# A decoder trunk in fp32 on one core: the address of three tiles in the SwiGLU, and the PSUM bank of one gate product

## The chip, the core and the metric

The kernel runs on one core of a Trainium2 chip. TensorE (PE) multiplies a moving tile of up to 512 columns with a stationary tile of 128 by 128 that a weight load (PEld) has put into it; results go to PSUM, here eight banks of 128 x 512 float32. VectorE (DVE), ScalarE (ACT) and GpSimd (POOL) work on tiles in SBUF, and DVE and ACT also read PSUM. DMAs are issued by SyncE's queue (SP), and some by POOL and ACT.

The metric is the device time of the whole program in microseconds. The median of three runs before the change is 1161.38 us (1160.37 to 1162.3).

## What is computed

One sequence of 512 tokens with 1,024 features passes a recurrent layer and an attention layer, each with a SwiGLU behind it. Only the recurrent mixer and the SwiGLU concern the change:

```python
def rg_lru(x, w_a, b_a, w_x, b_x, lam):
    ...
    r_gate = jax.nn.sigmoid(jnp.einsum('bshi,hij->bshj', xb, w_a.astype(jnp.float32)).reshape(B, S, C) + b_a.astype(jnp.float32))
    i_gate = jax.nn.sigmoid(jnp.einsum('bshi,hij->bshj', xb, w_x.astype(jnp.float32)).reshape(B, S, C) + b_x.astype(jnp.float32))
    log_a = -LRU_C * r_gate * jax.nn.softplus(-lam.astype(jnp.float32))
    a = jnp.exp(log_a)
    u = jnp.sqrt(-jnp.expm1(2.0 * log_a)) * (i_gate * x32)
...
def swiglu(h, w_in, w_out):
    g, u = jnp.split(h @ w_in, 2, axis=-1)
    return (jax.nn.silu(g) * u) @ w_out
```

The gates multiply each of eight blocks of 128 channels with a 128 x 128 matrix of its own, twice. The SwiGLU has a hidden width of 2,816.

## The kernel before

**Products.** The float32 result is kept by splitting each operand into a high and a low float32r part and adding three products: high with high, high with low, low with high. `mm3` (lines 164 to 168) issues them; its argument `w` is the stationary pair, `x` the moving pair. The profile names a matmul as out<-moving,stationary: `ps<-wh,T` has the tile `wh` moving and a slice of a tile `T` stationary.

**The recurrent layer.** Sixteen blocks of the input projection (`in_block`, 24 matmuls each) run in the order of `lru_order`: first the eight of the x branch (here projection blocks 0 to 7), then the eight of the y branch (8 to 15). Each takes a PSUM bank. `bank()` without a tag hands out the three banks `mm` and the bank `X` in turn; projection blocks 0, 1, 2 thus have `mm`, block 3 has `X`, and block 4 asks for `PT`, of which there are two. Blocks 5, 6, 7 have `mm`, block 8 `X` again. `x_block` (line 444) reads a projection block out of its bank with DVE, scales it into `xp`, and then come four taps of a convolution (lines 448 to 454: the first on ACT or POOL, three on DVE). `x_parts` splits the result into `xch` and `xcl`. `x_gates` (line 472) multiplies it with the two gate matrices, `pr` and `pi`, three matmuls each, and ACT reads them with a sigmoid (lines 482 and 484). Before the change `pr` has the bank `S` or `O` by turns and `pi` one of the two `PT`. The gates of blocks 0 and 1 follow projection block 5, those of 2 and 3 follow 6, those of 4 and 5 follow 8, those of 6 and 7 follow 9. ACT's sigmoids and exponentials are tied into runs (`act_order`), so that it changes its table seldom. The rest of this layer's order is made by a planner with estimates of its own, which may put parts of a projection block between the gates.

**The SwiGLU.** `swiglu` (line 578) is called twice, with the pool `ffn1` and with `ffn2`. The hidden blocks are computed by a scheme of seven products in place of eight (Strassen-Winograd), five times over (`ORDERS`): products with quarters of x as they lie in `xh` and `xl` (B11, B21, B22, T4), and three with sums and differences of x in the tiles `T1`, `T2`, `T3`. In each, slices of the x tile are stationary and the split weights `wh`, `wl` move; a product is 24 matmuls. Between them `out_block` (O) multiplies finished hidden chunks, `gh` and `gl` as moving tiles, with the output weights. At the end, T1 and T2 take the last hidden chunk, and eight blocks of 12 matmuls have them as moving tiles. In these stages the order of all five engines is written out by hand (`manual_schedule`).

**Where the tiles lie.** Pools lie one behind the other in a partition of SBUF, and in a pool the tiles lie in the order of their first call. Each number is an address in bytes in the partition, from the allocations:

| tile | begins at | remainder by 256 |
|---|---|---|
| h, xh, xl | 16,512; 32,896; 49,280 | 128 |
| wh and wl (three of 4,096 each) | 77,952; 90,240 | 128 |
| `gap` (128 bytes), ffn1 / ffn2 | 108,672 / 102,528 | 128 |
| T1, T2, T3 (8,192 each), ffn1 | 108,800; 116,992; 125,184 | 0 |
| T1, T2, T3, ffn2 | 102,656; 110,848; 119,040 | 0 |
| wt, the temporaries e, GA, GB, S1 | from 133,376 / 127,232 on | 0 |
| the norm's factors (`norm_factors`, 384 bytes), then S3, UB, rb, gh, gl | from 190,720 / 184,576 on | 128 from S3 on |

The tile `gap` is never read or written. It only takes up room.

Of the kernel before, what the change touches and what calls it, by code (L numbers as in the profile page):

```python
# [15 lines left out]
F32 = mybir.dt.float32  # L16
# [143 lines left out]
def trunk(tc, A, out):  # L160
# [3 lines left out]
    def mm3(ps, w, x, first, last, on=False):  # L164
        (wh, wl), (xh, xl) = w, x
        PE.matmul(ps, wh, xh, start=first, stop=False, skip_group_check=on)  # L166
        PE.matmul(ps, wh, xl, start=False, stop=False, skip_group_check=on)  # L167
        PE.matmul(ps, wl, xh, start=False, stop=last, skip_group_check=on)  # L168
# [55 lines left out]
    with tc.tile_pool(name="keep", bufs=1) as kp, tc.tile_pool(name="wts", bufs=3) as wp, \  # L224
# [6 lines left out]
        def bank(tag=None, name="ps"):  # L231
            tag = tag or next(rotation)
            return pp.tile([128, 512], F32, name=name, tag=tag, bufs={"mm": 3, "PT": 2}.get(tag, 1))
# [59 lines left out]
        def gain(c, k):  # L293
            return par[:, c + k:c + k + 1]
# [46 lines left out]
        with tc.tile_pool(name="lru", bufs=2) as lp, \  # L341
# [91 lines left out]
            def act_order(inst):  # L433

                for f in runs:
                    behind(tc, inst, f)
# [34 lines left out]

            def x_gates(b, xc, parts):
                c = slice(128 * b, 128 * b + 128)
                pr, pi = bank("SO"[b % 2]), bank("PT")
                for g, ps in enumerate((pr, pi)):
                    mm3(ps, (gwh[g][:, c], gwl[g][:, c]), parts, True, True)
                sl = slice(T * (b % 2), T * (b % 2) + T)
                if b % 2 == 0:
                    rate[b // 2] = lp.tile([128, 2 * T], F32, name="rate", bufs=4)
                    tau[b // 2] = lp.tile([128, 2 * T], F32, name="tau", bufs=4)  # L480
                r = rate[b // 2][:, sl]
                act_order(S.activation(r, pr, AF.Sigmoid, bias=gain(C_GA, b)))
                ig = lp.tile([128, T], F32, name="ig")
                act_order(S.activation(ig, pi, AF.Sigmoid, bias=gain(C_GX, b)))
                done.append(S.activation(tau[b // 2][:, sl], r, AF.Tanh, scale=sp4[:, b:b + 1]))
                V.tensor_tensor(gated[b], ig, xc, ALU.mult)
# [35 lines left out]
            for i, m in enumerate(lru_order):  # L522
                ps = first.pop(0) if first else in_block(p_in + i)

                if i in (5, 6, 8, 9):
                    for _ in range(2):
                        b = xs[0][0]
                        x_gates(*xs.pop(0))
                    if b % 4 == 3:
                        decays(b // 4)  # L530
                        decayed += range(b - 3, b + 1)
                        ready += 1
                if m < 8:
                    ys.append(y_block(m, ps))
                else:
                    xs.append(x_block(m - 8, ps))
                if i in (3, 5, 6, 8):
                    xs[:2] = [x_parts(*x) for x in xs[:2]]
                if i not in (6, 9):
                    for b in decayed[:2]:  # L540
                        recur(decayed.pop(0))
                while ys and ready == 2 and ys[0][0] < 8 - len(decayed):
                    y_gate(*ys.pop(0))
# [34 lines left out]
        def swiglu(fp, p, after, meanwhile=iter(())):  # L578
            ws.asp, ws.al = 2, 9
            temps = Temps(fp)  # L580
            fp.tile([128, 32], F32, name="gap", bufs=1)

            def chunk():
                return [fp.tile([128, 4, T], F32R, name=n, bufs=1) for n in ("gh", "gl")]
# [1 line left out]
            homes = {n: [x[:, 4 * k:4 * k + 4, 256 * t:256 * t + 256] for x in (xhs, xls)]  # L586
                     for n, k, t in (("B11", 0, 0), ("B21", 1, 0), ("B22", 1, 1), ("T4", 0, 1))}
            sums = [fp.tile([128, 4, T], F32R, name=f"T{i}", bufs=1) for i in range(1, 4)]
            for i, x in enumerate(sums):
                homes[f"T{i + 1}"] = [x[:, 2 * w:2 * w + 2].rearrange("q a (b t) -> q (a b) t", b=2) for w in range(2)]  # L590
            chunks = {}
# [233 lines left out]
        with tc.tile_pool(name="tables", bufs=1) as rp:  # L825
            rp = Pool(rp)
            with tc.tile_pool(name="ffn1", bufs=2) as fp:
                fp = Pool(fp)
                tables = []

                def make_tables():
                    tables.extend((yield from rotary(nc, A, rp, fp)))

                def after_f1(m, ps):
                    V.tensor_tensor(by_time(h[m]), by_time(h[m]), in_turn(ps), ALU.subtract)
                    split(h[m], gain(C_KV, m), xh[m], xl[m])
                    squares(m, Temps(fp))

                swiglu(fp, p_f1, after_f1, make_tables())


            with tc.tile_pool(name="att", bufs=2) as ap:
                ap = Pool(ap)
                attention(tc, A, ap, ws, dict(locals()))

        with tc.tile_pool(name="ffn2", bufs=2) as fp:
            fp = Pool(fp)

            def after_f2(m, ps):

                halves = [(slice(0, 2), nc.scalar), (slice(2, 4), nc.sync)]
                for c, queue in halves if m == 7 else [(slice(0, 4), nc.sync)]:
                    x = by_time(h[m])[:, :, c]
                    V.tensor_tensor(x, x, in_turn(ps)[:, :, c], ALU.subtract)
                    c = slice(128 * c.start, 128 * c.stop)
                    queue.dma_start(out[m][:, c], h[m][:, c])

            swiglu(fp, p_f2, after_f2)
# [534 lines left out]
```

## Time and profile before

| | |
|---|---|
| median of three runs | 1161.38 us |
| the profiled execution: time / its span | 1160.69 us / 1158.7 us |
| PE busy | 1150.0 us (99%) |
| DVE / ACT busy | 851.0 us (73%) / 622.9 us (54%) |
| granted clock of TensorE, mean | 1.00 |
| recurrent layer / first SwiGLU / attention / second SwiGLU | 0 to 156.5 / to 494 / to 824 / to 1158.7 us |

The span goes from the first to the last profiled instruction; the time of an execution holds some 2 us around it. Idle time of an engine counts only where the end waits for it, so the chain of work that ended last is read beside the busy times. A matmul's duration in the rows holds its way through the array, during which the next has begun already: how fast matmuls follow each other is read from their starts.

### The profile page before, as it was taken

What the parts mean: (1) busy time and instruction counts of PE and PEld (TensorE: products, weight loads), DVE (VectorE), ACT (ScalarE), POOL (GpSimd) and SP (SyncE); (2) the same over time, 40 slices, a digit from 0 to 9 for tenths busy, and PEclk for the clock granted to TensorE, in tenths of its full rate; (3) what the DMA queues carried; (4) which work ended last, traced back from release to release, by engine and by line L of the source; (5) the groups of instructions that cost most, each with busy time, mean ns of one, the idle gap of its engine ahead of it and who ended that gap; (6) DMA issues with size and microseconds to landing.
All of it is one profiled execution on the core that took longest, in us unless ns stands there. A gap on an engine that the chain in (4) does not pass through costs nothing.

```text
span 1158.7 us, 15131 instructions
## 1 busy us (share of the span) xinstructions
PE 1150.0 (99%) x5403; PEld 953.4 (82%) x5403; DVE 851.0 (73%) x1525; ACT 622.9 (54%) x901; POOL 187.7 (16%) x221
## 2 busy tenths in 40 slices
PE   9999999999999999999999999999999999999998
PEld 6788888888888888888888888798888888888886
DVE  8988688868777676887565667765888777676764
ACT  6797455553535353565555768665555435353531
POOL 4210010201001000020411234341102011010000
PEclk9999999999999999999999999999999999999999
DMA  7643366975666722432988658534668666657223
GB/s 243 154 113 110 103 226 161 241 202 153 185 167 180 183 74 82 122 108 88 222 185 174 156 104 198 119 74 110 222 160 231 193 162 188 171 167 194 76 76 124
DMA packets 92234, 179.61 MB, mean 155 GB/s; under 512 B 8704, under 2 KB 27008, under 8 KB 92160
## 3 DMA queue, kind: packets, MB, share of 16 engines
q1 hardware_dynamic: 72720, 130.80, 34.6%
q0 software_dynamic: 18864, 47.19, 23.2%
q8 instruction: 43, 0.70, 0.2%
q10 hardware_dynamic: 576, 0.66, 0.2%
q14 instruction: 31, 0.25, 0.1%
HBM read 164.99 MB, written 2.10 MB: 144 GB/s over the span
## 4 chain that ended last, share of the span: by engine, by line
PE 94%; DVE 2%; ACT 1%; issue 1%; POOL 0%; DMA 0%; SPq 0%; DVEq 0%; ACTq 0%
PE ps L168 25%; PE ps L167 25%; PE ps L166 25%; PE ps L1054 6%; PE ps L1055 6%; PE ps L1056 6%; PE ps L1222 1%; PE ps L1140 1%; DVE xc L454 1%; PE ps L299 0%; DMA wr<-in_w_in 0%; ACT pr L1208 0%; PE ps L1108 0%; ACT wh L117 0%; DVE wl L124 0%
## 5 line engine op out<-in xcount | busy, mean ns | idle before, releaser
L117 ACT CAST wh<-wr 128x1024 fp32r<-128x1024 f32 (+2 forms) x136 | 131.7, 970 | 134.9 <-PE ps L167 80.8
L168 PE MATMUL ps<-wh,xl 128*128 128x512 f32 x320 | 124.6, 390 | 0.0
L167 PE MATMUL ps<-wl,xh 128*128 128x512 f32 x320 | 124.6, 389 | 0.0
L166 PE MATMUL ps<-wh,xh 128*128 128x512 f32 x320 | 124.5, 389 | 0.0
L124 DVE TENSOR_TENSOR wl<-wr,wh 128x1024 fp32r<-128x1024 f32 (+2 forms) x93 | 100.4, 1083 | 18.2 <-ACT wh L117 18.1
L168 PE MATMUL ps<-gh,wl 128*128 128x512 f32 x288 | 112.2, 389 | 0.0
L167 PE MATMUL ps<-gl,wh 128*128 128x512 f32 x288 | 112.1, 389 | 0.0
L166 PE MATMUL ps<-gh,wh 128*128 128x512 f32 x288 | 112.0, 389 | 0.0
L653 POOL DMA_DIRECT2D S<-in_f_in x40 | 48.2, 1265 | 374.2 <-DMA S<-in_f_in 175.7
L166 PE MATMUL ps<-xh,wh 128*128 128x512 f32 x256 | 101.4, 398 | 0.3 <-ACT xh L277 0.3
L167 PE MATMUL ps<-xl,wh 128*128 128x512 f32 x256 | 100.1, 391 | 0.1
L168 PE MATMUL ps<-xh,wl 128*128 128x512 f32 x256 | 99.9, 390 | 0.0
L667 ACT CAST wh<-S 128x1024 fp32r<-128x1024 f32 x60 | 63.0, 1050 | 67.7 <-PE ps L168 28.1
L668 DVE TENSOR_TENSOR wl<-S,wh 128x1024 fp32r<-128x1024 f32 x60 | 73.2, 1222 | 30.3 <-ACT wh L667 30.3
L166 PE MATMUL ps<-wh,T 128*128 128x512 f32 x240 | 94.9, 396 | 0.0
L168 PE MATMUL ps<-wh,T 128*128 128x512 f32 x240 | 94.8, 395 | 0.0
L167 PE MATMUL ps<-wl,T 128*128 128x512 f32 x240 | 94.7, 395 | 0.0
L1054 PE MATMUL ps<-wh,xh 128*128 128x512 f32 x224 | 91.5, 408 | 0.0
L1056 PE MATMUL ps<-wh,xl 128*128 128x512 f32 x224 | 87.7, 391 | 0.0
L1055 PE MATMUL ps<-wl,xh 128*128 128x512 f32 x224 | 87.3, 390 | 0.0
L787 DVE TENSOR_TENSOR h<-h,ps 128x512 f32<-128x512 f32 x64 | 43.3, 685 | 49.6 <-PE ps L168 49.1
L166 PEld LDWEIGHTS ps<-wh,xh 128*128 128x128 f32 x320 | 60.1, 188 | 12.7
(284 smaller groups left out, 2673.2 us busy)
## 6 DMA issues: line engine op xcount, KB each, us to landing
S<-in_f_in SPq DMA_DIRECT2D x40, 512.0 KB, 6.7
S<-in_f_in POOLq DMA_DIRECT2D x40, 512.0 KB, 8.9
wr<-in_f_out SPq DMA_DIRECT2D x36, 512.0 KB, 5.0
wr<-in_w_q SPq DMA_DIRECT2D x28, 512.0 KB, 6.7
wl<-in_w_q POOLq DMA_DIRECT2D x28, 512.0 KB, 7.4
GA<-in_f_in SPq DMA_DIRECT2D x20, 512.0 KB, 4.7
GB<-in_f_in SPq DMA_DIRECT2D x20, 512.0 KB, 7.4
UB<-in_f_in SPq DMA_DIRECT2D x20, 512.0 KB, 5.2
```

What stands on the lines that cost most here:

```text
L117: nc.scalar.copy(hi[:, c], r[:, c])
L124: a = eng.tensor_tensor(lo[:, c], r[:, c], hi[:, c].bitcast(F32), ALU.subtract)
L166: PE.matmul(ps, wh, xh, start=first, stop=False, skip_group_check=on)
L167: PE.matmul(ps, wh, xl, start=False, stop=False, skip_group_check=on)
L168: PE.matmul(ps, wl, xh, start=False, stop=last, skip_group_check=on)
L653: nc.gpsimd.dma_start(c, p.part(1, q, n == "S1", i), accum_op=ALU.add)
L667: S.copy(hi, r)
L668: V.tensor_tensor(lo, r, hi.bitcast(F32), ALU.subtract)
L787: V.tensor_tensor(by_time(x), by_time(x), in_turn(ps), ALU.subtract)
L1054: PE.matmul(ps[t], xh[k][:, r], wh[:, c], start=k == 0, stop=False)
L1055: PE.matmul(ps[t], xh[k][:, r], wl[:, c], start=False, stop=False)
L1056: PE.matmul(ps[t], xl[k][:, r], wh[:, c], start=False, stop=k == 7)
```

## The change

Two edits. In the SwiGLU the tile `gap` is allocated behind T1 to T3 in place of ahead of them: the three tiles lie 128 bytes lower in both calls, and every tile behind the gap stays where it was. In the recurrent layer the second gate product `pi` of block 1 takes the bank `X` in place of a `PT`; the other seven keep `PT`.

```diff
             def x_gates(b, xc, parts):
                 c = slice(128 * b, 128 * b + 128)
-                pr, pi = bank("SO"[b % 2]), bank("PT")
+                pr, pi = bank("SO"[b % 2]), bank("X" if b == 1 else "PT")
                 for g, ps in enumerate((pr, pi)):
                     mm3(ps, (gwh[g][:, c], gwl[g][:, c]), parts, True, True)
...
             temps = Temps(fp)
-            fp.tile([128, 32], F32, name="gap", bufs=1)
 
             def chunk():
                 return [fp.tile([128, 4, T], F32R, name=n, bufs=1) for n in ("gh", "gl")]
...
             sums = [fp.tile([128, 4, T], F32R, name=f"T{i}", bufs=1) for i in range(1, 4)]
+            fp.tile([128, 32], F32, name="gap", bufs=1)
             for i, x in enumerate(sums):
```

No instruction is added or removed by either edit.

## The prediction

> **What bounds the kernel now.** I read the page first: its span, the busy line, the chain by engine.
>
> ```profile
> span 1158.7 us, 15131 instructions
> PE 1150.0 (99%) x5403; PEld 953.4 (82%) x5403; DVE 851.0 (73%) x1525; ACT 622.9 (54%) x901; POOL 187.7 (16%) x221
> PE 94%; DVE 2%; ACT 1%; issue 1%; POOL 0%; DMA 0%; SPq 0%; DVEq 0%; ACTq 0%
> ```
>
> TensorE is nearly never idle and carries the chain that ends last, so only two things can shorten the run: fewer idle stretches of PE, or matmuls that follow each other faster. A busy share can't show the second, so I next took the table by stretches, cut at the stages' borders: recurrent layer, first SwiGLU, attention, second SwiGLU. Its columns are the stretch, its length, then busy time and count of PE, weight loads, DVE, ACT, POOL.
>
> ```profile
> 0.00:156.50 156.50, 153.77 (x669) 124.64 (x670) 126.49 (x188) 110.09 (x149) 24.97 (x48) 1.00 0.48 136
> 156.50:494.00 337.50, 337.50 (x1481) 277.29 (x1480) 260.74 (x351) 160.79 (x207) 36.59 (x43) 1.00 0.61 170
> 824.00:1158.70 334.70, 331.04 (x1451) 271.61 (x1449) 242.49 (x305) 147.34 (x187) 35.22 (x40) 1.00 0.60 168
> ```
>
> In the first SwiGLU PE has no idle time at all, the granted clock is 1.00, and DVE and ACT have 77 and 177 us to spare. In the recurrent layer PE is idle for 2.7 us. The change touches these two places, and each needs a view of its own: groups by shape for the SwiGLU, the timeline for the recurrent layer.
>
> **Part 1: the tiles T1 to T3.** These are the matmul groups of the first SwiGLU (160 to 480 us), names as moving tile, then stationary tile; the last columns are busy time, mean ns of one, and idle time before.
>
> ```profile
> L168 PE MATMUL ps<-wh,xl 128*128 128x512 f32 x160 | 62.3, 390 | 0.0
> L167 PE MATMUL ps<-wl,xh 128*128 128x512 f32 x160 | 62.3, 389 | 0.0
> L166 PE MATMUL ps<-wh,xh 128*128 128x512 f32 x160 | 62.2, 389 | 0.0
> L167 PE MATMUL ps<-gl,wh 128*128 128x512 f32 x144 | 56.1, 389 | 0.0
> L166 PE MATMUL ps<-wh,T 128*128 128x512 f32 x120 | 47.5, 396 | 0.0
> L168 PE MATMUL ps<-wh,T 128*128 128x512 f32 x120 | 47.4, 395 | 0.0
> L167 PE MATMUL ps<-wl,T 128*128 128x512 f32 x120 | 47.3, 395 | 0.0
> L166 PE MATMUL ps<-T,wh 128*128 128x512 f32 x22 | 8.7, 395 | 0.0
> L166 PE MATMUL ps<-xh,wh 128*128 128x512 f32 x20 | 7.8, 389 | 0.0
> ```
>
> All have one shape and type, and none waited. Still every group with a T in it takes 395 or 396 ns, every other 389 or 390. Rows 1 to 3 and 5 to 7 share their moving tiles wh and wl, so T as the stationary operand costs 396, 395, 395 against 389, 390, 389: 6 ns. T as the moving operand (row 8, weights stationary) costs 395 against 389 for gl and xh: 6 ns again. What sets T apart is its address. By the allocations, xh, xl, wh, wl, gh and gl begin 128 bytes behind a multiple of 256, while T1, T2 and T3 begin on one, and all steps inside these tiles (512, 1,024, 2,048 bytes) keep that remainder. So each slow matmul joins remainder 0 with remainder 128, each quick one 128 with 128.
>
> A mean duration holds a tail that overlaps the next matmul, so I checked the starts at the border of the first T product, in PE's timeline (start, duration):
>
> ```profile
> 222.18 0.39 PE L166 MATMUL ps<-wh,xh 128*128 128x512 f32 x1
> ...
> 223.54 0.40 PE L166 MATMUL ps<-wh,T 128*128 128x512 f32 x1
> ...
> 227.27 0.39 PE L167 MATMUL ps<-wl,T 128*128 128x512 f32 x1
> ```
>
> Six starts before the border take 1.36 us, 227 ns each; sixteen behind it take 3.73 us, 233 ns each. The 6 ns are real time of PE.
>
> With the gap moved, T1 to T3 lie 128 bytes lower, at remainder 128; what lies above the gap stays. The number of matmuls that this touches is in the table by stretches for the tile T alone, one row for each SwiGLU:
>
> ```profile
> 157.00:488.00 331.00, 108.63 (x456) 85.88 (x456) 5.44 (x8) 4.30 (x6) 2.18 (x4) 1.00 0.61 169
> 824.00:1155.50 331.50, 108.64 (x456) 85.88 (x456) 6.51 (x10) 5.55 (x10) 2.18 (x4) 1.00 0.61 169
> ```
>
> By the loops 456 is 3 products x 5 orders x 24 matmuls = 360 with T stationary, and 8 blocks x 4 x 3 = 96 with T moving. The sum is 2 x 360 x 6 ns = 4.3 us and 2 x 96 x 6 ns = 1.2 us: **5.5 us**. With means rounded to whole ns, 5 to 7 ns are possible: 4.6 to 6.4 us. That the pair 128 with 128 would be worse than 390 ns is excluded by five groups at 389 or 390, and no group of this shape is below 389, so the bounds are a gain of 0 and of 6.4 us; I take 5.5, since the rows of the same stage show that pair directly.
>
> Does PE collect it? The list of waits shows who follows whom in these stages (total us, times, longest):
>
> ```profile
> ACT wh L667 <- PE ps L168: 120.3, 78, 2.0
> DVE h L787 <- PE ps L168: 49.1, 35, 2.0
> ```
>
> ACT splits the next weights only when PE releases a buffer, and DVE empties banks only when PE has filled them: both wait for PE, not PE for them. A T product (24 matmuls) gets 0.15 us shorter, far less than those waits of 1.5 us on average. ACT, DVE and the DMAs that touch T cost the same at either remainder (columns as above; the DMA rows end with size and us to landing):
>
> ```profile
> L743 DVE TENSOR_TENSOR gl<-gl,gh 128x512 fp32r<-128x512 f32 x32 | 20.6, 686 | 10.5 <-ACT gh L742 10.5
> L743 DVE TENSOR_TENSOR T<-T,T 128x512 fp32r<-128x512 f32 x8 | 5.0, 686 | 3.5 <-ACT T L742 3.5
> gl<-wt SPq DMA_DIRECT2D x96, 64.0 KB, 2.1
> T<-wt SPq DMA_DIRECT2D x24, 64.0 KB, 2.2
> ```
>
> One rule of the Trainium skill speaks against this part. The page "TensorE: Matmul & The Clock Gate", section "Step-by-step: what each phase is for", says that PE has two independent SBUF read ports and that "Loading the next tile's weights doesn't steal SBUF read bandwidth from the running matmul." By it the place of two operands relative to each other would not matter and this part would be worth 0; rows 1 to 3 against 5 to 7 disagree, by 6 ns.
>
> **Part 2: bank X for block 1's second gate.** PE's rows first, then DVE's and one of ACT, around an idle time of PE that a bank causes:
>
> ```profile
> 42.98 0.39 PE L166 MATMUL ps<-xh,wh 128*128 128x512 f32 x1
> 43.43 0.39 PE L168 MATMUL ps<-xh,wl 128*128 128x512 f32 x1
> 44.78 0.47 PE L166 MATMUL ps<-xch,gwh 128*128 128x512 f32 x1 [0.95 <-DVE xp L444]
> 50.30 0.39 PE L166 MATMUL ps<-xch,gwh 128*128 128x512 f32 x1
> 39.19 1.97 DVE L444 TENSOR_TENSOR xp<-ps,rb 128x512 f32<-128x512 f32 x2
> 43.55 1.08 DVE L444 TENSOR_TENSOR xp<-ps,rb 128x512 f32<-128x512 f32 x1
> 46.38 0.68 ACT L484 ACTIVATE ig<-ps,par 128x512 f32<-128x512 f32 x1
> ```
>
> The product at 44.78 is block 1's pi. Its bank is the PT that held projection block 4, which DVE reads from 43.55 to 44.63; PE goes on 0.15 us later. Without the wait it would have started 0.23 us behind 43.43: 1.12 us are lost. Bank X held projection block 3, read by 41.16 (the second of the two at 39.19). So X is free 1.8 us before PE reaches 42.98, whether pi comes before or after those three matmuls. The wait goes. X's next user is projection block 8, which stands 57 matmuls (13 us) behind block 1's pi; that bank's sigmoid takes 0.7 us and comes with block 1's others, so X is read long before. The gates of blocks 2 and 3, from 50.30 on, inherit the two PT banks: one read by 44.63, the other by block 0's sigmoid until 47.06.
>
> What is late next? PE, now 1.12 us ahead, meets the gates of blocks 6 and 7, whose banks ACT must have read:
>
> ```profile
> 57.24 0.62 ACT L282 CAST xch<-xc 128x512 fp32r<-128x512 f32 x1 [0.91 <-DVE xc L454]
> 68.95 1.28 ACT L482 ACT_TABLE_LOAD   x1
> 72.02 0.69 ACT L482 ACTIVATE rate<-ps,par 128x512 f32<-128x512 f32 x1
> 73.42 0.39 PE L166 MATMUL ps<-xch,gwh 128*128 128x512 f32 x1
> ```
>
> Block 7's first gate, now at 73.42, takes the bank that ACT reads until 72.71. ACT has no idle time between 57.24 and there, and at 57.24 it waited for DVE, which is itself busy throughout. So ACT does not follow when PE comes earlier. Ahead by 1.12, PE would be there at 72.30 but can go on only at 72.71 + 0.15 = 72.86: 0.56 us stay. Part 2 gives **0.56 us**, between 0 (DVE and ACT shifted against it) and 1.12 (ACT also earlier).
>
> **The sum.** 5.5 + 0.56 = 6.1 us. The profiled execution took 1160.69 us, 2.0 more than its span, and becomes 1154.6; the median shown, 1161.38, lies 0.7 above it and becomes **1155.3**. Differences under 0.2% (2.3 us) can't be told from no change here.
>
> **The rivals.** *The address is not the cause.* The slices of T are packed 1,024 bytes apart and those of xh 2,048, so T could be slow by its pattern; then only part 2 acts: 1160.8. For it: T is the only tile at remainder 0 in those rows, so remainder and tile can't be parted there. Against it: as a moving operand T is read in rows like gl's, and is slow too. This is also where the skill's rule on the two ports leads. 6%.
>
> *One side only.* The clash might stay in one role, say the 192 matmuls with T moving (weights loaded while a long T row is read): 1155.3 + 1.2 = 1156.5; or in the 720 others: 1159.6. Nothing speaks for it but that the two are different reads. 7%, mostly the first.
>
> *Slower: the plan of the recurrent layer changes.* Its order comes from a planner that sees pi earlier and may order ACT anew. ACT is the late engine there, and each switch between sigmoid and exponential costs 1.28 us (68.95). A pi put behind its projection block's remaining 21 matmuls (21 x 0.227 = 4.8 us) passes that lateness on to the gates of blocks 6 and 7, and two needless switches there and back add 4 x 1.28 = 5.1. Together 9.9 us against the 5.5 of part 1: 1161.4 + 4.4 = 1165.8. It makes the kernel slower from 7.8 us lost on. Against it: the instructions and their dependencies stay, and the sigmoids are tied into runs by hand. 2%.
>
> **How the numbers follow.** Forecast 85%, 1155.3; its own range is 1155.3 plus the 0.9 us by which part 1 may fall short, plus 0.56 if part 2 gives nothing, and about 1 us by which medians of runs shown differ: to 1157.8. Downward 0.9, 0.56 and 0.5: 1153.3. The first form of the second rival lies inside. 1153.3 to 1157.8 leaves out some 12%. Faster by over 0.2% (below 1159.1): the forecast and the larger part of the second rival, 90%; within: first rival and the rest, 8%; slower: 2%.
>
> **What would show it.** Part 1: all groups with T fall from 395 or 396 to 389 or 390 ns, both SwiGLU stretches get 2.7 us shorter, PE stays without idle time there. T at 395 makes the first rival right; T,wh alone at 395 the second. Part 2: no idle time of PE near 43 to 45 us; in its place some 0.5 us before the gates near 72 us, released by ACT's L482. If PE is idle longer than 1.1 us in the recurrent layer, or ACT loads more tables, the plan changed. The forecast is wrong if PE's idle time in a SwiGLU grows by what its matmuls gain.

## The result and the profile after

The changed kernel takes 1155.06 us (median of 6 runs, 1154.27 to 1156.07) against 1161.41 us before: ratio 0.9947, 95% interval 0.9934 to 0.996. That is 6.35 us less by the two medians and 6.2 by the ratio, where 6.1 were forecast (1155.3).

The page of the profile after, the lines that answer to the first fence of the prediction:

```profile
span 1152.3 us, 15131 instructions
PE 1143.5 (99%) x5403; PEld 952.1 (83%) x5403; DVE 851.4 (74%) x1525; ACT 622.9 (54%) x901; POOL 187.4 (16%) x221
PE 92%; DVE 3%; ACT 3%; issue 1%; POOL 1%; DMA 0%; ACTq 0%; DVEq 0%; POOLq 0%
```

The number of instructions is the same, the busy times of DVE, ACT and POOL differ by 0.4 us at most, and PE has 6.5 us less. Where this was gained needs fixed marks. Each stage begins with a norm, and DVE reads the norm's sums at line 301, once a stage. These are its rows in DVE's timeline (start, duration; the rows between them are left out), before and then after:

```profile
21.04 0.16 DVE L301 TENSOR_SCALAR nrv<-ps 128x4 f32<-128x4 f32 x1
157.50 0.15 DVE L301 TENSOR_SCALAR nrv<-ps 128x4 f32<-128x4 f32 x1
495.98 0.17 DVE L301 TENSOR_SCALAR msv<-ps 128x8 f32<-128x8 f32 x1 [0.48 <-PE ps L299]
825.96 0.15 DVE L301 TENSOR_SCALAR nrv<-ps 128x4 f32<-128x4 f32 x1
```

```profile
21.25 0.16 DVE L301 TENSOR_SCALAR nrv<-ps 128x4 f32<-128x4 f32 x1
157.23 0.15 DVE L301 TENSOR_SCALAR nrv<-ps 128x4 f32<-128x4 f32 x1
492.62 0.17 DVE L301 TENSOR_SCALAR msv<-ps 128x8 f32<-128x8 f32 x1 [0.22 <-PE ps L299]
822.61 0.15 DVE L301 TENSOR_SCALAR nrv<-ps 128x4 f32<-128x4 f32 x1
```

The differences of these starts, and of the last to the end of the span, are the stretches: recurrent layer 136.46 and 135.99 us, first SwiGLU 338.48 and 335.39, attention 329.98 and 329.99, second SwiGLU 332.74 and 329.69. So the two SwiGLUs gave 3.09 and 3.05 us, the recurrent layer 0.47, attention nothing. The first mark itself comes 0.21 us later after the change; 6.6 us of gain behind it are therefore 6.4 in the span.

The groups of the first SwiGLU after (160 to 480 us; moving tile, then stationary tile; busy us, mean ns, idle before):

```profile
L167 PE MATMUL ps<-wl,xh 128*128 128x512 f32 x160 | 62.2, 389 | 0.0
L168 PE MATMUL ps<-wh,xl 128*128 128x512 f32 x160 | 62.2, 389 | 0.0
L166 PE MATMUL ps<-wh,T 128*128 128x512 f32 x120 | 46.7, 389 | 0.0
L167 PE MATMUL ps<-wl,T 128*128 128x512 f32 x120 | 46.7, 389 | 0.0
L166 PE MATMUL ps<-T,wh 128*128 128x512 f32 x27 | 10.5, 389 | 0.0
```

T is no longer to be told from its neighbours, as stationary or as moving tile, and PE still has no idle time in front of any of them.

In the recurrent layer the wait of 1.12 us is gone. PE's timeline after: the end of block 1's pr, its pi, the next projection block, and then the gates of blocks 6 and 7:

```profile
42.96 0.39 PE L168 MATMUL ps<-xch,gwl 128*128 128x512 f32 x1
43.19 0.39 PE L166 MATMUL ps<-xch,gwh 128*128 128x512 f32 x1
...
43.87 0.39 PE L166 MATMUL ps<-xh,wh 128*128 128x512 f32 x1
...
70.84 0.39 PE L168 MATMUL ps<-xh,wl 128*128 128x512 f32 x1
71.18 0.50 PE L166 MATMUL ps<-xch,gwh 128*128 128x512 f32 x1
...
72.44 0.39 PE L168 MATMUL ps<-xch,gwl 128*128 128x512 f32 x1
72.95 0.50 PE L166 MATMUL ps<-xch,gwh 128*128 128x512 f32 x1
```

pi follows pr at once (0.23 us between starts; the planner now puts all of the next projection block behind it). But 0.34 and 0.51 us lie between the starts at 70.84 and 71.18 and at 72.44 and 72.95, where 0.23 is the pace: 0.11 and 0.28 us are lost again. ACT's row of the same moment shows to whom: the bank of block 7's pr is read until 72.21 + 0.69 = 72.90, and PE goes on at 72.95. Block 6's pr at 71.18 waits in the same way for the sigmoid on line 482 that ACT ends at 71.13.

```profile
72.21 0.69 ACT L482 ACTIVATE rate<-ps,par 128x512 f32<-128x512 f32 x1
```

### The profile page after: what moved, and what is told of

It reads as the page before. It is cut to its first block, busy times and chain, and to the rows that moved or that the text cites. A ratio compares the mean times of both kernels' runs of the same rounds, so it can differ in the third digit from the quotient of the medians.

```text
span 1152.3 us, 15131 instructions
## 1 busy us (share of the span) xinstructions
PE 1143.5 (99%) x5403; PEld 952.1 (83%) x5403; DVE 851.4 (74%) x1525; ACT 622.9 (54%) x901; POOL 187.4 (16%) x221
## 4 chain that ended last, share of the span: by engine, by line
PE 92%; DVE 3%; ACT 3%; issue 1%; POOL 1%; DMA 0%; ACTq 0%; DVEq 0%; POOLq 0%
PE ps L167 24%; PE ps L168 24%; PE ps L166 24%; PE ps L1054 6%; PE ps L1055 6%; PE ps L1056 6%; DVE xc L454 1%; PE ps L1222 1%; PE ps L1140 1%; ACT wh L117 0%; PE ps L299 0%; DMA wr<-in_w_in 0%; ACT pr L1208 0%; DVE xp L444 0%; DVE xl L278 0%
## 5 line engine op out<-in xcount | busy, mean ns | idle before, releaser
L166 PE MATMUL ps<-wh,T 128*128 128x512 f32 x240 | 93.4, 389 | 0.0
L168 PE MATMUL ps<-wh,T 128*128 128x512 f32 x240 | 93.4, 389 | 0.0
```

## The experiments

Ten kernels. The table gives for each profiled execution the four stretches as above, and how long the accumulating DMA for projection block 14 took from issue to landing, which part 2 leads to. The time is the median of the runs, or the one run. In brackets stands the 95% interval of its ratio to runs of the kernel before that were taken along with it (their medians are 1161.41 to 1161.85 us). The stretches go by starts that are not rounded, so the last digit can differ from the rows above; the mark is on line 302 in e3 and e4, which have one line more.

| kernel | recurrent layer | first SwiGLU | attention | second SwiGLU | landing, block 14 | time, us (interval of the ratio) |
|---|---|---|---|---|---|---|
| before | 136.46 | 338.48 | 329.98 | 332.75 | 6.5 | 1161.41 |
| after | 135.99 | 335.38 | 329.99 | 329.68 | 6.5 | 1155.06 (0.9934 to 0.996) |
| e1_gap_only | 136.46 | 335.37 | 329.96 | 329.68 | 6.4 | 1154.83 (0.9929 to 0.9956) |
| e2_bank_only | 137.43 | 338.48 | 329.97 | 332.77 | 7.9 | 1161.55 (0.9988 to 1.0005) |
| e3_all_at_0 | 136.68 | 335.38 | 330.02 | 329.63 | 7.2 | 1154.65 (0.9926 to 0.9954) |
| e4_mixed_other_way | 137.46 | 338.48 | 330.04 | 332.73 | 8.0 | 1161.7 (0.9986 to 1.0005) |
| e5_gap_64 | 136.36 | 338.44 | 330.06 | 332.68 | 6.9 | 1162.3 (one run) |
| e6_gap_256 | 136.21 | 335.38 | 330.02 | 329.69 | 6.7 | 1154.13 (one run) |
| e7_chunks_at_0 | 137.05 | 338.35 | 329.99 | 332.64 | 7.6 | 1161.43 (0.9988 to 1.0006) |
| e8_bank_for_7 | 137.38 | 335.38 | 329.96 | 329.68 | 7.9 | 1155.77 (one run) |
| e9_block14_dve | 136.59 | 335.38 | 330.99 | 329.67 | none | 1154.57 (0.9928 to 0.9954) |
| e10_both | 136.66 | 335.39 | 329.95 | 329.68 | none | 1155.09 (0.9931 to 0.9959) |

The SwiGLU columns know two values only, 338.4 and 335.4, and 332.7 and 329.7, within 0.15 us. The times of kernels with the same SwiGLU stretches scatter by 0.9 to 1.6 us and would not have shown this so sharply; a stretch between two marks of one trace does.

### Each part alone: e1_gap_only, e2_bank_only

```diff
-                pr, pi = bank("SO"[b % 2]), bank("X" if b == 1 else "PT")
+                pr, pi = bank("SO"[b % 2]), bank("PT")
```

That is e1, against the kernel after. e2 is the kernel before with the line of the bank as changed.

> The gap moved, all eight pi in PT as before. If the pair of remainders sets the pace of the matmuls (main theory), the nine groups with T go to 389 ns and the time to 1161.4 - 5.5 = 1155.9 us, ratio 0.9953; PE waits 1.1 us at 44 us as before. If most of the gain came from the bank (rival), the time stays above 1159.

> The bank changed, the gap where it was. T groups stay at 395 or 396 ns. If ACT, late until the gates of blocks 6 and 7, takes back half of the stall (main theory), the time is 1161.4 - 0.5 = 1160.9 us, ratio 0.9996, and PE waits some 0.5 us before 73 us. If the whole stall goes (rival), 1160.3.

The gap alone has the whole gain as far as the time can tell: ratio 0.9942 (0.9929 to 0.9956), and both SwiGLU stretches as in the changed kernel. The bank alone has a ratio of 0.9996, and its interval holds 1: in the time it can't be told from nothing. Its profiled execution is even 0.97 us longer in the recurrent layer, though the wait at 44 us is gone. PE's timeline of e2 says why:

```profile
96.76 0.39 PE L167 MATMUL ps<-xl,wh 128*128 128x512 f32 x1
98.33 0.50 PE L168 MATMUL ps<-xh,wl 128*128 128x512 f32 x1 [1.19 <-DMA wl<-in_w_in]
```

PE waits 1.2 us for the low part of the weights of projection block 14. ACT and a DMA of POOL's queue make it: the DMA accumulates the weights from HBM onto what ACT wrote. The view of line 121 (89 to 99 us) has this one DMA, first e1, then e2:

```profile
L121 POOL DMA_DIRECT2D wl<-in_w_in x1: 850/850/850, 89.6 to 89.6; - x1
DMA to landing us min/median/max: 6.4/6.4/6.4
```

```profile
L121 POOL DMA_DIRECT2D wl<-in_w_in x1: 852/852/852, 90.3 to 90.3; - x1
DMA to landing us min/median/max: 7.9/7.9/7.9
```

From the mark on line 301 it is issued after 68.8 us in all of the first ten kernels of the table, whether PE has waited for the bank or not. It follows ACT: in the changed kernel ACT writes this tile until 89.74, and POOL, which waited for that, issues the DMA at 90.03. It lands 6.4 to 8.0 us later. This is the third limit of this stage, behind the bank and ACT. In the kernels with bank X the recurrent layer grows with the landing, us for us: 6.5 gives 135.99, 6.7 gives 136.21, 6.9 gives 136.36, 7.2 gives 136.68, 7.6 gives 137.05, 7.9 gives 137.38 and 137.43. With the old bank 6.4 and 6.5 give 136.46 (the bank binds) and 8.0 gives 137.46 (the landing binds, e4). So with the landings seen here bank X saves at most 0.5 us, and by these rows nothing when that DMA takes 7.0 us or longer. Even in the profile of the changed kernel, where it lands early, it holds PE up a little: the first matmul with that low part is longer than its neighbours, and the next starts 0.31 us behind it in place of 0.23.

```profile
96.64 0.48 PE L168 MATMUL ps<-xh,wl 128*128 128x512 f32 x1
96.95 0.39 PE L166 MATMUL ps<-xh,wh 128*128 128x512 f32 x1
```

### Which addresses clash: e3_all_at_0, e4_mixed_other_way

```diff
+        kp.tile([128, 32], F32, name="low")
         h = [kp.tile([128, T], F32, name=f"h{k}") for k in range(KB)]
```

e3 adds these 128 unused bytes to the kernel after, e4 to the kernel before.

> The changed kernel with 128 unused bytes ahead of all tiles: T, xh, xl, wh, wl, gh, gl and the recurrent layer's tiles all at remainder 0 by 256, no pair mixed. If only the pair counts (main theory), every group of 512 columns in the SwiGLU is at 389 or 390 ns and the time is 1155 us, as changed. If a tile at remainder 0 is slow by itself (rival), all of them go to 395 or 396: some 4,000 matmuls x 6 ns = 24 us more, 1179.

> The kernel before with 128 unused bytes ahead of all tiles: T at remainder 128, all that it is multiplied with at 0. By the pair of remainders (main theory) the T groups stay at 395 or 396 ns and the rest at 389: 1161.4 us as before. If remainder 0 is slow by itself (rival), T falls to 389 only where it alone counts, and the groups without T, now 0 with 0, rise to 395: above 1175. If 128 bytes lower or higher is all that T needs (rival), T is at 389 and the time 1156.

Groups of the first SwiGLU, e3 and then e4:

```profile
L166 PE MATMUL ps<-wh,xh 128*128 128x512 f32 x160 | 62.2, 389 | 0.0
L166 PE MATMUL ps<-gh,wh 128*128 128x512 f32 x144 | 56.0, 389 | 0.0
L166 PE MATMUL ps<-wh,T 128*128 128x512 f32 x120 | 46.7, 389 | 0.0
```

```profile
L166 PE MATMUL ps<-wh,xh 128*128 128x512 f32 x160 | 62.3, 389 | 0.0
L166 PE MATMUL ps<-gh,wh 128*128 128x512 f32 x144 | 56.0, 389 | 0.0
L166 PE MATMUL ps<-wh,T 128*128 128x512 f32 x120 | 47.5, 396 | 0.0
```

In e3 all these tiles lie on multiples of 256, T at the very addresses where it was slow before, and all are quick: remainder 0 is not slow by itself, nor is T. In e4 T lies at 128, where it is quick in the changed kernel, and is slow, because now all others lie at 0. Both stretches agree with the kernels after and before to 0.05 us. It is the pair that counts.

### Another tile: e7_chunks_at_0

```diff
             def plain_parts():
+                fp.tile([128, 32], F32, name="gap2", bufs=1)
                 chunks[0] = chunk()
```

> The changed kernel with 128 unused bytes ahead of gh and gl, which go to remainder 0; T stays at 128. By the pair of remainders (main theory) the gh and gl groups, moving against weights at 128, go from 389 to 395 ns: 864 x 6 ns = 5.2 us more, 1160.3 us. If the slowness belonged to T and its packing (rival), they stay at 389 and the time at 1155.

```profile
L166 PE MATMUL ps<-gh,wh 128*128 128x512 f32 x144 | 56.8, 395 | 0.0
L166 PE MATMUL ps<-wh,T 128*128 128x512 f32 x120 | 46.7, 389 | 0.0
```

gh and gl, never slow before, are slow in T's place, as moving tiles against weights at 128. The two stretches are 2.97 and 2.96 us longer than after, 5.9 for 864 matmuls, and the time is back at 1161.43 us. The rival that T's packing is the cause falls with this and with e3.

### How fine and how far: e5_gap_64, e6_gap_256

```diff
+            fp.tile([128, 16], F32, name="gap1", bufs=1)
             sums = [fp.tile([128, 4, T], F32R, name=f"T{i}", bufs=1) for i in range(1, 4)]
-            fp.tile([128, 32], F32, name="gap", bufs=1)
+            fp.tile([128, 16], F32, name="gap", bufs=1)
```

This is e5. e6 puts `fp.tile([128, 64], F32, name="gap1", bufs=1)` there and leaves `gap` at 32.

> 64 of the 128 bytes below T, 64 above: T at remainder 192, the rest as changed. If only the half of 256 bytes in which a tile begins counts, T stays at 389 ns (1155 us). If every difference of the remainders costs alike, T is at 395 (1160.5). If the cost grows with the overlap of unlike halves, about half of it, 392 (1158).

> 256 more bytes below T: T, gh and gl at remainder 384 by 512, and still 128 by 256, against wh and wl at 128 by 512. If the period is 256 bytes (main theory) all groups stay at 389 ns and the time at 1155 us. If it is 512 or more (rival), T and gh, gl go to 395: (912 + 864) x 6 ns = 10.7 us more, 1166.

e5, then e6:

```profile
L166 PE MATMUL ps<-wh,T 128*128 128x512 f32 x120 | 47.5, 396 | 0.0
L166 PE MATMUL ps<-T,wh 128*128 128x512 f32 x20 | 7.9, 394 | 0.0
L168 PE MATMUL ps<-T,wl 128*128 128x512 f32 x19 | 7.5, 392 | 0.0
L167 PE MATMUL ps<-T,wh 128*128 128x512 f32 x19 | 7.4, 389 | 0.0
```

```profile
L166 PE MATMUL ps<-gh,wh 128*128 128x512 f32 x144 | 56.0, 389 | 0.0
L166 PE MATMUL ps<-wh,T 128*128 128x512 f32 x120 | 46.7, 389 | 0.0
```

64 bytes of difference cost as much as 128 where T is stationary. Where it moves, two of the three groups pay 5 and 3 ns and the third nothing; why they differ stays open. The half of 256 bytes in which a tile begins is therefore not the rule. 256 bytes of difference cost nothing. Of the differences tried, 64 and 128 cost, 0 and 256 don't; 32 and 192 were not tried.

### Does anything lie behind the bank: e8_bank_for_7, e9_block14_dve, e10_both

```diff
-                pr, pi = bank("SO"[b % 2]), bank("X" if b == 1 else "PT")
+                pr, pi = bank("X" if b == 7 else "SO"[b % 2]), bank("X" if b == 1 else "PT")
```

That is e8. e9 instead has the weights' low part of projection block 14 made by DVE, with no DMA:

```diff
-    add_pieces([A["w_in"][m] for m in lru_order[4:15]], "dma", 3)
-    add_pieces([A["w_in"][m] for m in lru_order[15:]])
+    add_pieces([A["w_in"][m] for m in lru_order[4:14]], "dma", 3)
+    add_pieces([A["w_in"][m] for m in lru_order[14:]])
```

e10 has both edits.

> The changed kernel with bank X also for pr of block 7. If the wait before 73 us is for the bank that ACT reads late (main theory), it goes there, and a shorter wait of some 0.3 us turns up at block 7's pi, whose PT ACT reads until 73.5; the time moves by less than 0.3 us. If PE waits there for the split of the convolution's result (rival), the wait stays at block 7's pr.

> The changed kernel with the low part of projection block 14's weights made by DVE, as for blocks 10 and 13, in place of ACT and an accumulating DMA of POOL's. If the landing of that DMA is what takes back the gain of the bank (new theory), PE has no idle time near 97 us, and from the norm's first product to the next norm's it takes 135.9 us, as in the best profile of the changed kernel and 0.5 less than the 136.40 before the change; the time is 1154.5 to 1155.1 us. If DVE, then 1.2 us busier, is late instead (rival), PE waits for hgl or y after 100 us and that stretch is 136.4 or longer.

> As e9_block14_dve, and bank X also for pr of block 7. If the late banks of blocks 6 and 7 and the landing for block 14 are all that PE waits for behind 45 us (new theory), there is no idle time of PE from 22 us to the next norm, and the stretch between the norms' first products is 135.3 to 135.7 us, up to 1.1 below 136.40; the time is 1154 to 1155 us. If the wait only moves to the next late split (rival), PE is idle somewhere between 73 and 120 us and the stretch is 135.9 or longer.

PE's timeline, e8: the end of block 7's pr and its pi, then the wait at block 14; and below, from e9:

```profile
72.62 0.40 PE L168 MATMUL ps<-xch,gwl 128*128 128x512 f32 x1
72.86 0.39 PE L166 MATMUL ps<-xch,gwh 128*128 128x512 f32 x1
...
73.31 0.40 PE L168 MATMUL ps<-xch,gwl 128*128 128x512 f32 x1
73.71 0.50 PE L166 MATMUL ps<-xch,gwh 128*128 128x512 f32 x1
...
98.15 0.50 PE L168 MATMUL ps<-xh,wl 128*128 128x512 f32 x1 [1.25 <-DMA wl<-in_w_in]
```

```profile
108.47 0.50 PE L168 MATMUL ps<-hgh,wl 128*128 128x512 f32 x1 [0.41 <-DVE wl L124]
```

e8: block 7's pr (72.86) follows without loss, and its pi loses 0.17 us (0.40 between starts). So the wait before 73 us was for the bank that ACT reads late. But what this gained was lost at 98.15, with 7.9 us of landing. In e9 the wait for the landing is gone, and in its place PE waits at 108.47 for DVE, which ends that split of the output weights 1.4 us later than in the changed kernel, counted from the mark: 136.59, not 135.9. The rival was right here, though it had named other tiles of DVE's (hgl or y). In e10 PE waits 0.48 us at 109.01 for the same split, and the stretch is 136.66, not 135.3 to 135.7: there too the rival was right, and shorter waits at the gates of blocks 6 and 7 remain. None of the versions beats the changed kernel by more than the runs scatter. (e9's attention took 1.0 us longer in its one profile. Of this, 0.71 us is a wait of PE at 577.68 for the landing of another accumulating DMA, `wl<-in_w_q`, which the profile of the changed kernel doesn't have.)

## Why the prediction was right

**Part 1, mechanism.** Right, and shown: whether the two tiles begin at the same remainder by 256 or not sets the pace. e3, e4 and e7 take the tile's place and the tile itself out of the question, and the first rival (6%) with them. The second (7%) falls with the change itself, where both roles gained; in e7 moving tiles alone are slow, and in e5 the stationary role pays its full 6 to 7 ns.

**Part 1, size.** 5.5 us were forecast and 6.14 came (3.09 and 3.05), inside the bounds of 4.6 to 6.4. The term was mis-sized by its rounding, and by counting the T groups alone. The table by stretches for the tile T shows the first half of it. After the change:

```profile
157.00:485.00 328.00, 105.80 (x456) 85.59 (x456) 5.17 (x7) 4.30 (x6) 2.18 (x4) 1.00 0.61 171
```

Against 108.63 us before, that is 2.83 us a SwiGLU, 5.7 in both, 6.2 ns for each of the 912 and not 6.0. The remaining 0.4 us lies beside T's rows, and the starts show where. In the first SwiGLU T's own matmuls give 2.85 of the 3.10 us (unrounded) by their starts. The 14 matmuls that stand directly before a run of T products have both their own tiles at 128, and still the next start came 232 ns behind theirs; after the change it comes 226.5 ns behind: 0.08 us. The other 0.17 us is spread over the remaining matmuls, some tenths of a ns each.

**Does PE collect it?** Yes: idle time in front of every group above is 0.0 as before, and ACT's and DVE's waits for PE shrank a little, as they should when PE is the quicker one:

```profile
ACT wh L667 <- PE ps L168: 116.0, 77, 1.9
DVE h L787 <- PE ps L168: 47.0, 35, 2.0
```

They were 120.3 and 49.1 us.

**Part 2.** The first two steps were right: X was free, the wait of 1.12 us went, and ACT's late read of the bank for block 7's pr gave part of it back, at 72.95 us. Counted by starts against a pace of 0.227 us, with the matmul behind each late one, which starts 0.08 to 0.11 us late as well, the old wait cost 1.20 us and the two new ones 0.62 (0.23 at block 6's pr, which the prediction did not name, and 0.39 at block 7's): 0.58 us remain, where 0.56 were forecast. The stretch in the one profile of the changed kernel shows 0.47, because the landing for block 14 already takes some of it there. Wrong is the step "What is late next?": it stopped at the gates of blocks 6 and 7. Behind them stands the landing of the DMA for block 14, at a time that PE does not set and that differs by 1.6 us between executions, so the 0.56 could hold only where it lands earlier than in any profile with bank X here. Over many runs part 2 is worth, by the ten profiles, between 0 and 0.5 us; e2's ratio of 0.9996 fits that, and its interval, as wide as 1.0 us to either side, doesn't narrow it. That the sum came out so close is luck in part: part 1 was 0.6 us too small, and part 2 is probably some tenths too large.

**The rival on the slow side** did not occur: the planner moved three matmuls, ACT's busy time is 622.9 us in both pages, and the clock stayed at 1.00.

**The rule of the Trainium skill** in "TensorE: Matmul & The Clock Gate", section "Step-by-step: what each phase is for", that loading the next weights takes no SBUF read bandwidth from the running matmul, doesn't fit these runs without a condition: 389 ns when the two tiles begin at the same remainder by 256 (0 and 0, 128 and 128, 384 and 128), 395 or 396 when they differ by 128. The border in the first SwiGLU before the change shows such a load, PE's row and then the weight load's:

```profile
223.31 0.40 PE L168 MATMUL ps<-wh,xl 128*128 128x512 f32 x1
223.32 0.19 PEld L166 LDWEIGHTS ps<-wh,T 128*128 128x128 f32 x1
```

The running matmul has both its tiles at 128, but while it runs a slice of T is loaded, and it is one of the 14 slow ones above. This speaks for a clash of the moving tile with the load of the next stationary one. It does not settle it: the last matmul of a run of T products, during which a tile at 128 is loaded, is slow too (235 to 236 ns to the next start), and in e5, with 64 bytes of difference, the matmul before a T product is quick (226 ns). That the two reads meet in the memory is an inference.

## What to carry to other kernels

When PE is busy throughout, compare the mean duration of matmul groups of one shape before looking for idle time: a group that is 1.5% slower than its neighbours with no wait in front of it is a question about the operands' addresses, and a gap of 128 bytes may answer it, as it did here. When a wait is taken out, list every later instruction of that engine with less slack than the gain, landings of DMAs among them, and not the first alone. Take stretches between marks of one trace for what is smaller than the scatter of the runs.

## What was not expected of the hardware

A difference of 64 bytes between the two tiles costs as much as one of 128 when the odd tile is stationary (396 ns against 389), but less when it moves (394, 392 and 389 in three groups). And one accumulating DMA of 512 KB, issued by POOL at the same point of the kernel, took 6.4 to 8.0 us to land in ten profiled executions, with no change to its own issue; what it shared the time with was not separated.
